# Moving the four feature-major projections of the gated linear attention from behind the delta rule's chain to between its silu gate and the first branch's norm

## The chip, the cores and the metric

One core of a Trainium2 chip. The metric is the device time of one execution in microseconds, the median of the runs shown. Engines are named as in the profile: PE (TensorE matmuls), DVE (VectorE), ACT (ScalarE), POOL (GpSimd), SP (the queue that issues most DMAs).

## The reference, cut to what matters

Two stacked blocks of two layers each, batch 1, 256 tokens, width 1024, all in float32. The change lies in the token mixing of the first block, which both of its layers run:

```python
def token_mixing(x, w_in, ...):
    h = (x @ w_in).astype(jnp.float32)
    h_rw, h_gla, h_gdn, h_gate = _split(h, GROUP_SPLITS)
    o_rw = rwkv7_time_mix(h_rw, ...)
    o_gla = gla_mix(q, k, v, gk_lo, gate, ...)         # the five parts of h_gla
    o_gdn = gated_deltanet_mix(qkv, a_in, b_in, gate, ...)
    branches = jnp.stack([o_rw, o_gla, o_gdn], axis=2)
    proj = jnp.einsum('btnc,ncd->btnd', branches, w_branch)
    gates = jax.nn.sigmoid(h_gate).reshape(B, T, N_BRANCH, D_MODEL)
    return jnp.sum(gates * proj, axis=2) @ w_o

def gla_mix(q, k, v, gk_lo, gate, gk_w2, gk_b, norm_g):
    log_a = jax.nn.log_sigmoid(gk_lo @ gk_w2 + gk_b) / GLA_GATE_NORM
    # per chunk of 64, b = cumsum(log_a):
    #   att[i, j] = sum_d q[i, d] k[j, d] exp(b[i, d] - b[j, d]),  j <= i
    #   o = att @ v + (q * exp(b)) @ S ;  S = S * exp(b_end) + (k * exp(b_end - b))^T v
    return _rms_norm(o, norm_g) * jax.nn.silu(gate)

def gated_deltanet_mix(...):
    # per chunk: t_inv = (I + lower)^-1 ; u = t_inv @ (v beta) ; w = t_inv @ (k beta exp(g))
    # chain over 4 chunks: v_new = u - w @ S ; o = (q exp(g)) @ S + att @ v_new ; S = ...
    return _rms_norm(o, norm_g) * jax.nn.silu(gate)
```

The second block (attention, then HGRN, each with a swiglu) is modulated by `silu(c) @ ada_w`, a matrix product that needs nothing of the first block.

## The kernel before

**Products.** Each float32 product is three matmuls of a high and a low part (hi·hi, hi·lo, lo·hi). The activations are split once per stage (`xh`, `xl`). Weights come in units of 128x1024 floats: SP loads `wr`, ACT makes `wh` (L78), DVE makes `wl` (L79). There are 4 buffers for `wr`, 4 for `wh` and 3 for `wl`. Feature-major projections ("fm", `fm_tile`, L102, L103 and L105) take one unit for one output tile of 128 features by 256 tokens, 24 matmuls. Token-major projections ("tm", L178 to L180) give 128 tokens by 512 features; a unit lasts for 12 matmuls when both halves of the tokens use it.

**Order.** The text gives an order of emission; a list scheduler then orders the instructions on each engine, so that two neighbouring steps of the text are interleaved where their dependences allow. Each engine runs its own list strictly in order.

**The stage.** `token_mix` emits in this order: 15 fm tiles for RWKV with its inverse and chain; 12 fm tiles for the delta rule (d15 to d26); `gd_mid`, in which the inverse of the delta rule is made (rounds on DVE L449/L450, transposes L455, copies on ACT L453 and L467 to tile `iz`, then four groups of L487 on PE with DVE between them); gate projections; the tm projection of the delta rule's silu gate (`silu_gate`, L951 to L953); the RWKV norm `rw_post` (DVE L697 to L704, PE L712/L713, DVE L714) and its output projection `proj(l, 0, ytm)`; the chain of the delta rule over four chunks (`gd_chain`, L895 to L927 with the head norm L937 to L944); then the gated linear attention: four fm tiles l27 to l30 (k and q, two tiles each, copied to `Lk`, `Lq` by ACT L962), `gl_mid`, the tm projection of v (`Lv`, L1201), and so on.

`gl_mid` works in two halves, j = 0 and 1. A half starts with L996 on PE (the decay gate, from data that are there long before) and the products of q and k (L1014, read by DVE L1015); DVE takes differences of the running sum (14 instructions, L975/L976), ACT one Exp of 128x1792 (L977), DVE multiplies by q and k (14 instructions, L981, tile `Lex`), and then, for seven levels, PE multiplies (L1025, four small matmuls into two `pt` tiles) and DVE copies the result under a mask into `Lat` (L1032, four of them). The `pt` tiles have two buffers, so level n+1 of L1025 cannot start before L1032 has read level n.

**Fill.** The projection of the second block's modulation is split into 48 doses. A dose is four matmuls (L1389) from a tile loaded ahead (`fr`) or from two `wr` tiles, with L1395, L1408 and L1414 behind every second one. Named places of the text (`spot`) fetch a tile ("f"), give a dose from a fetched one ("d") or give a number of doses. The places in question: `sg` f, `post` d, `chain` f, `l27` d, `l28` f, `l30` d, `lg` f, `g1` d, `p2` f, `glo` d, `wo0` f, `wo` d and 2 more.

Of the kernel before, what the change touches and what calls it, by code (L numbers as in the profile page):

```python
# [17 lines left out]
P = 128  # L18
T = 256
# [341 lines left out]
for _k, _w in ROWS:  # L361
# [3 lines left out]
FMT = (["lora"] + [f"{c}{p}" for p in range(4) for c in "krv"] + ["g0", "misc"]  # L365
       + [f"G{c}{h}" for c in "kqv" for h in range(4)] + ["Lk0", "Lq0", "Lk1", "Lq1"])
# [30 lines left out]
class Mix(Core):  # L397
# [557 lines left out]


    def gl_begin(self):
        self.lq = {c: self.t([P, 2, T], f"L{c}", bufs=1) for c in "kq"}

    def gl_tile(self, f, ps):  # L960
        j = int(f[2])
# [115 lines left out]
class Block(Mix):  # L1077
# [62 lines left out]
    def token_mix(self, l, pool, ln):  # L1140
        nc, tc = self.nc, self.tc
        self.wfm, self.wtm, self.layer = self.a["wfm"][l], self.a["wtm"][l], l
        self.merged, self.gt = {}, {}
        new = lambda n, **k: tc.tile_pool(name=f"{n}{l}", bufs=1, reuse_waits="tile", **k)
        with new("mg") as self.mg:
            self.pre = {(0, h): self.t([P, 2, 512], f"gate0{h}", pool=self.mg) for h in range(2)}
            self.vnat = self.t([P, 2, 512], "vnat", pool=self.mg)
            self.ytm = self.t([P, 2, 512], "ytm", pool=self.mg)
            self.load_params(l)
            with new("gd") as self.gd:  # L1150
                gw = ExitStack()
                self.gw = gw.enter_context(new("gw", side="right"))
                with new("gp") as self.gp:
                    self.rw_begin()
                    with new("mp") as self.mx:
                        for i in range(15):
                            self.rw_tile(i, self.fm_tile(i))
                            self.spot(f"r{i}")
                            if i == 14:
                                self.gates(0, self.mg, (0,))  # L1160
                    with new("mi") as self.mx:
                        self.rw_inverse()
                        self.rw_chain()
                with new("la") as self.late:
                    self.rt = self.t([P, NROW], "rt", pool=self.late)
                    self.gx = self.t([P, 1024], "gx", pool=self.late)
                    nc.gpsimd.dma_start(self.rt, self.a["row"][l:l + 1].broadcast_to([P, NROW]))
                    nc.gpsimd.dma_start(self.gx, self.a["gx"][l])
                    gs = self.t([P, 2, 512], "gsg", pool=self.late)
                    self.gd_begin()  # L1170
                    for i in range(15, 27):
                        self.gd_tile(FMT[i], i, self.fm_tile(i))
                        if i == 24:
                            self.gd_decay()
                        if i == 26:
                            self.gd_scale()
                        self.spot(f"d{i}")
                        if i == 18:
                            self.gates(0, self.mg, (1,))
                    with new("mj") as self.mx:  # L1180
                        self.gd_mid()
                    gw.close()
                    self.spot("mid")
                    self.gates(2, self.late)
                    self.spot("g2")
                    self.tm(self.wtm, 2 * KD, 1, self.xh, self.xl, KD, lambda n, t, ps: self.silu_gate(ps, gs[:, t], "gdn_g"), last=0)
                    self.spot("sg")
                    self.rw_post()
                    self.spot("post")
                    self.proj(l, 0, self.ytm)  # L1190
                    with new("dc") as self.dc:
                        self.gd_chain(lambda t, o: self.head_norm(o, gs[:, t], gs[:, t]))
                        with new("ml") as self.mx:
                            self.spot("chain")
                            self.gl_begin()
                            for i in range(27, 31):
                                self.gl_tile(FMT[i], self.fm_tile(i))
                                self.spot(f"l{i}")
                            self.gl_mid()
                            v = self.t([P, 2, 512], "Lv")  # L1200
                            self.tm(self.wtm, 0, 1, self.xh, self.xl, KD, lambda n, t, ps: nc.scalar.copy(v[:, t], ps), last=0)  # L1201
                            gl = self.t([P, 2, 512], "gsl")
                            self.tm(self.wtm, KD, 1, self.xh, self.xl, KD, lambda n, t, ps: self.silu_gate(ps, gl[:, t], "gla_g"), last=0)
                            self.spot("lg")
                            self.gates(1, self.mg)
                            self.spot("g1")
                            self.gl_out(lambda t: v[:, t], lambda t, o: self.head_norm(o, gl[:, t], gl[:, t]))
                            self.proj(l, 2, gs)
                            self.spot("p2")
                            self.spot("glo")  # L1210
                            self.proj(l, 1, gl)
            mh, ml = self.new_x("m")
            self.to_fm(lambda t: self.merged, mh, ml, scale=0.5)
        self.x_load(pool())
        self.ln_begin(ln)
        self.spot("wo0")
        self.tm(self.a["wo"][l], 0, 2, mh, ml, KD, self.ln_sink, cut=True)
        self.spot("wo")
        self.ln_end()
# [868 lines left out]
```

## Time and profile before

| what | value |
|---|---|
| median of 3 runs | 2869.21 us (2865.56 to 2870.39) |
| the profiled execution's own time | 2880.61 us |
| its span (first to last instruction) | 2878.4 us |
| mean granted clock of PE | 0.981 of full |
| PE busy | 2785.6 us, 97% of the span |
| DVE busy | 1879.9 us, 65% |
| ACT busy | 1299.4 us, 45% |
| chain that ended last | PE 85%, DVE 9%, ACT 3%, DMA 2% |

How to read it: the span less PE's busy time is what PE waits, 93 us over the whole execution. A matmul at half clock counts as busy, so time lost to the clock does not show in that difference; it shows in the granted clock of a stretch. In the first layer the silu gate of the delta rule ends at about 433 us of the span, the gated linear attention's last part at about 620; in the second layer it is the stretch from 1324 to 1510. All times below are of the profiled execution.

### The profile page before, as it was taken

To read this page: it belongs to the slowest core of one execution; us is meant where nothing else is said; L and a number is where in the kernel's file an instruction comes from. 1 tells how busy PE (TensorE), PEld (TensorE's weight loads), DVE (VectorE), ACT (ScalarE), POOL (GpSimd) and SP (SyncE) were. 2 spreads that over 40 slices of the span, in tenths; PEclk is the share of its full clock that TensorE was granted. 3 is DMA by queue.
4 is the path that set the end of the run, shared out by engine and by line. 5 is a ranking of instruction groups with operands and counts; after the bars stand their busy time and mean duration, and the time that the engine had idled before them with its cause. 6 is when DMAs were issued, how large, how long until landed. Compare 5 with 4: busy or idle time off the path is not lost.

```text
span 2878.4 us, 47877 instructions
## 1 busy us (share of the span) xinstructions
PE 2785.6 (97%) x18788; PEld 2457.3 (85%) x18788; DVE 1879.9 (65%) x3880; ACT 1299.4 (45%) x2040; POOL 202.8 (7%) x320
## 2 busy tenths in 40 slices
PE   8999999999999999999999998999999999999998
PEld 8978887669978987887778986798999888898897
DVE  5658885676556658877677657686444327799665
ACT  4436543435434435633444534564333225564543
POOL 0000220020000001211010001200000001000000
PEclk9999999899999999989999999999999999999999
DMA  7555333465556555323357556202322323214554
GB/s 251 182 196 172 115 127 103 140 210 188 185 205 216 183 186 188 128 97 118 117 181 240 180 179 218 100 8 89 97 98 93 125 93 117 76 57 155 182 182 151
DMA packets 117009, 426.64 MB, mean 148 GB/s; under 512 B 13600, under 2 KB 14112, under 8 KB 115760
## 3 DMA queue, kind: packets, MB, share of 16 engines
q1 hardware_dynamic: 115168, 419.01, 43.7%
q0 software_dynamic: 1472, 4.51, 0.5%
q8 instruction: 148, 2.42, 0.3%
q14 instruction: 77, 0.63, 0.1%
q10 hardware_dynamic: 144, 0.07, 0.0%
HBM read 420.36 MB, written 3.18 MB: 147 GB/s over the span
## 4 chain that ended last, share of the span: by engine, by line
PE 85%; DVE 9%; ACT 3%; DMA 2%; issue 1%; POOL 0%; DVEq 0%; POOLq 0%; ACTq 0%; SPq 0%
PE ps L102 13%; PE ps L103 13%; PE ps L105 12%; PE ps L179 10%; PE ps L178 10%; PE ps L180 10%; PE pc L487 2%; DVE wl L79 2%; PE pc L1389 1%; PE pc L1643 1%; PE pt L243 1%; PE pt L1025 1%; PE pt L1627 1%; ACT wh L78 1%; PE pt L1830 1%
## 5 line engine op out<-in xcount | busy, mean ns | idle before, releaser
L79 DVE TENSOR_TENSOR wl<-wr,wh 128x1024 fp32r<-128x1024 f32 x658 | 809.6, 1232 | 558.2 <-issue 199.4
L78 ACT CAST wh<-wr 128x1024 fp32r<-128x1024 f32 x658 | 688.2, 1048 | 670.8 <-PE ps L180 307.7
L102 PE MATMUL ps<-xh,wh 128*128 128x256 f32 x3280 | 940.3, 288 | 10.6 <-ACT xh L247 4.8
L103 PE MATMUL ps<-xh,wl 128*128 128x256 f32 x3280 | 933.9, 286 | 3.1 <-DVE wl L79 3.1
L105 PE MATMUL ps<-xl,wh 128*128 128x256 f32 x3168 | 902.6, 285 | 0.4 <-DVE xl L254 0.3
L102 PEld LDWEIGHTS ps<-xh,wh 128*128 128x128 f32 x3280 | 634.2, 193 | 21.8 <-ACT wh L78 6.0
L103 PEld LDWEIGHTS ps<-xh,wl 128*128 128x128 f32 x3280 | 633.8, 193 | 9.5 <-DVE wl L79 4.3
L105 PEld LDWEIGHTS ps<-xl,wh 128*128 128x128 f32 x3168 | 608.4, 192 | 5.9 <-issue 4.1
L178 PE MATMUL ps<-wh,xh 128*128 128x512 f32 (+1 forms) x624 | 248.5, 401 | 4.2 <-ACT wh L78 2.8
L179 PE MATMUL ps<-wl,xh 128*128 128x512 f32 (+1 forms) x624 | 249.5, 400 | 0.6 <-DVE wl L79 0.5
L180 PE MATMUL ps<-wh,xl 128*128 128x512 f32 (+1 forms) x624 | 247.2, 398 | 0.0
L180 PE MATMUL ps<-wh,hl 128*128 128x512 f32 (+1 forms) x616 | 228.7, 371 | 0.0
L179 PE MATMUL ps<-wl,hh 128*128 128x512 f32 (+1 forms) x616 | 228.5, 371 | 0.0
L178 PE MATMUL ps<-wh,hh 128*128 128x512 f32 (+1 forms) x616 | 228.2, 371 | 0.0
L178 PEld LDWEIGHTS ps<-wh,xh 128*128 128x128 f32 x624 | 119.4, 192 | 33.1 <-ACT wh L78 3.2
L179 PEld LDWEIGHTS ps<-wl,xh 128*128 128x128 f32 x624 | 119.9, 192 | 26.8 <-DVE wl L79 3.8
L180 PEld LDWEIGHTS ps<-wh,xl 128*128 128x128 f32 x624 | 119.8, 192 | 23.4 <-issue 1.1
L151 ACT ACTIVATE th<-ps 128x256 f32<-128x256 f32 x154 | 59.2, 384 | 171.0 <-PE ps L105 160.1
L178 PEld LDWEIGHTS ps<-wh,hh 128*128 128x128 f32 x616 | 116.1, 189 | 22.4 <-DVE g L154 0.4
L179 PEld LDWEIGHTS ps<-wl,hh 128*128 128x128 f32 x616 | 116.0, 188 | 21.6
L180 PEld LDWEIGHTS ps<-wh,hl 128*128 128x128 f32 x616 | 116.0, 188 | 21.4
L155 ACT CAST hh<-g 128x256 fp32r<-128x256 f32 x154 | 62.5, 406 | 116.9 <-DVE g L154 116.9
(565 smaller groups left out, 3736.7 us busy)
## 6 DMA issues: line engine op xcount, KB each, us to landing
wr<-in_up SPq DMA_DIRECT2D x264, 512.0 KB, 3.5
wr<-in_down SPq DMA_DIRECT2D x132, 512.0 KB, 3.4
wr<-in_wtm SPq DMA_DIRECT2D x72, 512.0 KB, 3.4
wr<-in_wfm SPq DMA_DIRECT2D x62, 512.0 KB, 4.0
fr<-in_ada SPq DMA_DIRECT2D x23, 1024.0 KB, 5.3
wr<-in_ada SPq DMA_DIRECT2D x38, 512.0 KB, 4.3
wr<-in_wbr SPq DMA_DIRECT2D x24, 512.0 KB, 3.5
wr<-in_whfm SPq DMA_DIRECT2D x24, 512.0 KB, 3.4
```

The lines of the kernel that those rows point to most:

```text
L78: on_act = nc.scalar.copy(hi, raw)
L79: on_dve = nc.vector.tensor_tensor(lo, raw, hi.bitcast(F32), ALU.subtract)
L102: nc.tensor.matmul(o, hi[:, w], xh[:, k], start=k == 0, stop=False)
L103: nc.tensor.matmul(o, lo[:, w], xh[:, k], start=False, stop=False)
L105: nc.tensor.matmul(o, hi[:, w], xl[:, k], start=False, stop=k == nk - 1)
L151: nc.scalar.activation(th, pa[:, :T], AF.Tanh, scale=0.5)
L155: nc.scalar.copy(hh[:, m], g)
L178: nc.tensor.matmul(o, xh[:, k, s], h, start=first, stop=False)
L179: nc.tensor.matmul(o, xh[:, k, s], l, start=False, stop=False)
L180: nc.tensor.matmul(o, xl[:, k, s], h, start=False, stop=end)
L243: nc.tensor.transpose(pt[:, j, t * P:t * P + P], self.cols(src(t), t, k + j), self.ident)
L487: nc.tensor.matmul(ps[:, 64 * u:64 * u + 64], lhs[:, u], rhs[:, u], start=True, stop=True)
```

## The change

The four fm tiles l27 to l30, with their spots, are emitted between spot `sg` and `rw_post` and no longer behind spot `chain`. Since the tiles `Lk` and `Lq` then live longer, they are taken from the pool `late`, which is open over both places, and no longer from the pool of the attention stage.

```diff
     def gl_begin(self):
-        self.lq = {c: self.t([P, 2, T], f"L{c}", bufs=1) for c in "kq"}
+        self.lq = {c: self.t([P, 2, T], f"L{c}", bufs=1, pool=self.late) for c in "kq"}
...
                     self.spot("sg")
+                    self.gl_begin()
+                    for i in range(27, 31):
+                        self.gl_tile(FMT[i], self.fm_tile(i))
+                        self.spot(f"l{i}")
                     self.rw_post()
                     self.spot("post")
                     self.proj(l, 0, self.ytm)
...
                             self.spot("chain")
-                            self.gl_begin()
-                            for i in range(27, 31):
-                                self.gl_tile(FMT[i], self.fm_tile(i))
-                                self.spot(f"l{i}")
                             self.gl_mid()
```

No instruction is added or taken away but for the doses' places. What the scheduler makes of it is shown at three places of the first layer; the second layer has the same pattern.

**Place A, PE, the inverse of the delta rule.** `pc` of L487 is its result, `iz` what it waits for, `ps_4856` the last tile of the silu gate. Before:

```order
L180 MATMUL ps_4856<-wh_4911,xl_2233 128x512
L712 MATMUL pt_4983<-gx_3669,g_537_3203 128x512
L713 MATMUL pt_4983<-gx_3669,misc_3241 128x512
L712 MATMUL pt_5031<-gx_3669,g_537_3203 128x512
L713 MATMUL pt_5031<-gx_3669,misc_3241 128x512
L487 MATMUL pc_4649<-iz_810_4635,int_4480 128x64 x8
L1414 MATMUL pt_5040<-cst,row_4473 128x128 x4
L243 MATMUL pt_5048<-cst,ytm_2280 128x128 x4
L487 MATMUL pc_4660<-iym_4648,ixb_4641 128x64 x8
```

After (`ps_4941` is tile l27, `ps_4984` tile l28):

```order
L180 MATMUL ps_4856<-wh_4911,xl_2233 128x512
L102 MATMUL ps_4941<-xh_2232,wh_4942 128x256
...
L105 MATMUL ps_4941<-xl_2233,wh_4942 128x256
L1414 MATMUL pt_4978<-cst,row_4473 128x128 x2
L487 MATMUL pc_4649<-iz_810_4635,int_4480 128x64 x8
L1414 MATMUL pt_4978<-cst,row_4473 128x128 x2
L102 MATMUL ps_4984<-xh_2232,wh_4985 128x256
...
L103 MATMUL ps_4984<-xh_2232,wl_4986 128x256
L487 MATMUL pc_4660<-iym_4648,ixb_4641 128x64 x8
L105 MATMUL ps_4984<-xl_2233,wh_4985 128x256
```

The 24 matmuls of l27 now stand ahead of the first L487 where the two pairs of L712/L713 stood; l28 to l30 stand behind it, between the four groups of L487, and L712/L713 follow them.

**Place B, PE, the levels of `gl_mid`, j = 0.** `ps_5830` and `ps_5831` are tiles of a tm projection, `pt` the results of a level. Before:

```order
L178 MATMUL ps_5830<-wh_5850,xh_2232 128x512
L179 MATMUL ps_5830<-wl_5851,xh_2232 128x512
L1025 MATMUL pt_5551<-Lex_5511 128x64 x2
L1025 MATMUL pt_5552<-Lex_5511 128x64 x2
L180 MATMUL ps_5830<-wh_5850,xl_2233 128x512
...
L180 MATMUL ps_5830<-wh_5850,xl_2233 128x512
L1025 MATMUL pt_5561<-Lex_5511 128x64 x2
L1025 MATMUL pt_5562<-Lex_5511 128x64 x2
L178 MATMUL ps_5831<-wh_5850,xh_2232 128x512
```

After (`fr` is a dose's tile):

```order
L178 MATMUL ps_5902<-wh_5904,xh_2232 128x512
L1025 MATMUL pt_5540<-Lex_5500 128x64 x2
L1025 MATMUL pt_5541<-Lex_5500 128x64 x2
L1025 MATMUL pt_5550<-Lex_5500 128x64 x2
L1025 MATMUL pt_5551<-Lex_5500 128x64 x2
L1025 MATMUL pt_5560<-Lex_5500 128x64 x2
L1389 MATMUL pc_6055<-fr_6243,adac 32x512
L1025 MATMUL pt_5561<-Lex_5500 128x64 x2
L179 MATMUL ps_5819<-wl_5840,xh_2232 128x512
L1025 MATMUL pt_5570<-Lex_5500 128x64 x2
```

Where seven tm matmuls stood between one level and the next, the levels now follow one another with one dose matmul between them, and the next tm row needs the weight part `wl_5840`.

**Place B, DVE.** `wl` is a low weight part, `Lat` the result of a level, `hss` to `rsy` the head norm of the delta rule's last chunk. Before:

```order
L981 TENSOR_TENSOR Lex_5511<-Lex_5511,Lk_5336 128x2x64
L1032 COPY_PREDICATED Lat_5485<-lvm,pt_5541 128x64 x2
L1032 COPY_PREDICATED Lat_5485<-lvm,pt_5542 128x64 x2
L1039 TENSOR_TENSOR Lke_5613<-Lke_5613,Lk_5336 128x128
L79 TENSOR_TENSOR wl_5869<-wr_5870,wh_5868 128x1024
L1032 COPY_PREDICATED Lat_5485<-lvm,pt_5551 128x32x2 x2
L1032 COPY_PREDICATED Lat_5485<-lvm,pt_5552 128x32x2 x2
L79 TENSOR_TENSOR wl_5887<-wr_5888,wh_5886 128x1024
```

After:

```order
L79 TENSOR_TENSOR wl_5822<-wr_5823,wh_5821 128x1024
L917 TENSOR_TENSOR go_947_5399<-goo_5442,pc_5437 64x512
L981 TENSOR_TENSOR Lex_5500<-Lex_5500,Lq_4940 128x128
...
L213 SCALAR_TENSOR_TENSOR rsy_5453<-rst_5454,rsy_5453 128x4
L1032 COPY_PREDICATED Lat_5474<-lvm,pt_5531 128x64
L944 SCALAR_TENSOR_TENSOR gsg_3672<-go_947_5399,rsy_5453,gsg_3672 128x128 x4
...
L1032 COPY_PREDICATED Lat_5474<-lvm,pt_5550 128x16x4 x2
L79 TENSOR_TENSOR wl_5840<-wr_5841,wh_5839 128x1024
L1032 COPY_PREDICATED Lat_5474<-lvm,pt_5551 128x16x4 x2
L1032 COPY_PREDICATED Lat_5474<-lvm,pt_5560 128x8x8 x2
```

Between two weight parts DVE now has the 14 L981, the head norm of the last chunk (L939 to L944) and the copies of two and a half levels; before, the head norm stood ahead of L981, and a weight part followed each level.

## Rows read from the trace of the kernel before

**Rows 1.** The page: its first line, and PE (busy us, share, instructions).

```profile
span 2878.4 us, 47877 instructions
PE 2785.6 (97%) x18788; PEld 2457.3 (85%) x18788; DVE 1879.9 (65%) x3880; ACT 1299.4 (45%) x2040; POOL 202.8 (7%) x320
```

**Rows 2.** Waits of PE, 390:620, then 1290:1520; us in total, times, longest.

```profile
PE pc L487 <- ACT iz L467: 5.0, 1, 5.0
PE pt L1025 <- ACT Lv L1201: 0.3, 1, 0.3
...
PE pc L487 <- ACT iz L467: 5.1, 1, 5.1
```

**Rows 3.** Timeline of PE from the silu gate's end: start, us, instruction, [wait, releaser].

```profile
433.07 0.39 PE L180 MATMUL ps<-wh,xl 128*128 128x512 f32 x1
433.30 1.02 PE L712 MATMUL pt<-gx,g 128*128 128x512 f32 x2
...
436.36 1.12 PE L713 MATMUL pt<-gx,misc 32*128 32x512 f32 x2
442.44 3.65 PE L487 MATMUL pc<-iz,int 128*128 128x64 f32 x16 [4.96 <-ACT iz L467]
```

**Rows 4.** Stretches: length, PE, PEld, DVE, ACT, POOL busy (x), PEclk, DMA share, GB/s.

```profile
442.44:449.07 6.63, 6.63 (x32) 6.63 (x32) 3.19 (x6) 2.09 (x4) 0.00 (x0) 0.50 0.01 2
534.40:551.30 16.90, 16.90 (x44) 10.83 (x43) 5.21 (x15) 6.65 (x10) 0.00 (x0) 0.50 0.20 66
...
1424.00:1432.00 8.00, 8.00 (x34) 5.15 (x33) 2.69 (x11) 2.35 (x4) 0.00 (x0) 0.79 0.21 68
```

**Rows 5.** Timeline of PE: neighbouring fm matmuls, and a level between tm matmuls.

```profile
654.06 0.28 PE L102 MATMUL ps<-xh,wh 128*128 128x256 f32 x1
654.18 0.28 PE L103 MATMUL ps<-xh,wl 128*128 128x256 f32 x1
...
532.03 0.50 PE L179 MATMUL ps<-wl,xh 128*128 128x512 f32 x1
532.46 0.66 PE L1025 MATMUL pt<-Lex 64*128 64x64 f32 x4
533.05 0.50 PE L180 MATMUL ps<-wh,xl 128*128 128x512 f32 x1
```

**Rows 6.** Timeline of DVE in the head norm and in `gl_mid`, j = 0.

```profile
506.73 0.68 DVE L939 TENSOR_REDUCE hss<-sgt 128x4 f32<-128x512 f32 x1
...
508.38 0.15 DVE L211 TENSOR_TENSOR rst<-rsy 128x4 f32<-128x4 f32 x1
...
508.65 0.15 DVE L212 SCALAR_TENSOR_TENSOR rst<-rst,hss 128x4 f32<-128x4 f32 x1
...
512.82 1.14 DVE L944 SCALAR_TENSOR_TENSOR gsg<-go,rsy,gsg 128x128 f32<-128x128 f32 x4
...
516.90 2.35 DVE L79 TENSOR_TENSOR wl<-wr,wh 128x1024 fp32r<-128x1024 f32 x2
519.17 0.28 DVE L981 TENSOR_TENSOR Lex<-Lex,Lq 128x128 f32<-128x128 f32 x1
...
522.00 0.73 DVE L1032 COPY_PREDICATED Lat<-lvm,pt 128x64 f32<-128x64 uint8 x4
```

**Rows 7.** Groups of ACT by form, 433:620: busy us, mean ns, idle before.

```profile
L977 ACT ACTIVATE Lex<-Lex 128x1792 f32<-128x1792 f32 x2 | 3.4, 1698 | 0.0
L903 ACT COPY gvn<-pc 64x512 f32<-64x512 f32 x4 | 2.3, 580 | 4.6 <-PE pc L901 4.6
```

**Rows 8.** Timeline of PE: a dose in the next norm, that norm's longest wait, and the HGRN head's end.

```profile
640.63 1.42 PE L1389 MATMUL pc<-wr,adac 128*32 128x512 f32 x5
...
648.01 0.58 PE L102 MATMUL ps<-xh,wh 128*128 128x256 f32 x1 [2.78 <-ACT xh L247]
...
2639.63 1.05 PE L243 MATMUL pt<-cst,o 128*128 128x128 f32 x4 [1.96 <-DVE o L1854]
...
2641.68 0.63 PE L178 MATMUL ps<-wh,xo 128*128 128x512 f32 x1
```

## The prediction

> **What bounds the kernel now.** I read the page first: PE is busy 97% of the span [rows 1], so a change that adds and removes no matmul can move the time in three ways only: PE waits for something else, the same matmuls run at another clock, or small matmuls break runs of large ones in other places. Then the waits of PE in the stage. In the first layer's stage there is one large wait, 5.0 us, at the first L487 of the delta rule's inverse, released by ACT's copy to `iz`; the second layer has the same with 5.1; the levels of `gl_mid` (L1025) wait only 0.3 us [rows 2]. The timeline shows the first: the silu gate's last matmul starts at 433.07, L712/L713 fill until 437.5, and L487 starts at 442.44 [rows 3]. Last I read the granted clock by stretches, because a slow matmul counts as busy: after that wait PE runs at 0.50, the lower level of 1.2 GHz, for 6.63 us, all of it busy, which loses 3.3 us; and from 534.40 to 551.30, at the end of `gl_mid` and behind it, it runs 16.90 us at 0.50, which loses 8.5. The second layer loses less there: 8.00 us at 0.79, which is 0.21 x 8.00 = 1.7 us [rows 4].
>
> **The change, part by part.** All sums stand against the profiled execution, 2880.61 us (span 2878.4 [rows 1], 2.2 outside it). The median of the runs shown is 2869.21, so a result of mine is multiplied by 2869.21/2880.61 = 0.996.
>
> *The wait at the inverse (place A).* What frees it is DVE's chain of rounds and ACT's copies; the order on DVE and ACT ahead of `iz` is the same in both kernels, so L487 stays at about 442.4. In front of it PE had L712/L713, from 433.30 to about 437.5, 4.2 us [rows 3]. Now it has l27 alone: 24 fm matmuls at 0.12 us from one start to the next [rows 5] are 2.9, with two L1414 about 3.2. The wait grows by 1.0, in each of the two layers: +2.1 us. l28 to l30 stand behind L487, where PE waited for nothing, and the L712/L713 that they push back are no longer cover for anything. DVE's L714, which now follows them, releases L243; I put 0.2 a layer on that, from nothing to the 0.7 that one such DVE instruction takes by the like of L939 [rows 6]: +0.4. The half clock behind the wait stays, since the wait does: 0.
>
> *Small groups between large matmuls.* A tm matmul in front of a level takes 0.43 us from start to start instead of 0.23 (532.03 to 532.46 [rows 5] against 433.07 to 433.30 [rows 3]). With l27 to l30 joined to other fm and the levels joined to each other, the order has 121 passages from large to small matmuls or back in the first layer's stage before and 115 after, and 125 and 116 in the second. At 0.1 each, half of those 0.20, the 15 fewer give −1.5 (0 to −3).
>
> *The levels of `gl_mid` (place B).* Before, `gd_chain` ran over the fm tiles and the levels over the tm projection of v. Now the chain and the first half of `gl_mid` share one place, the chain uses up v, and the levels stand together, with DVE's weight part `wl_5840` behind two and a half of them. I count from PE's last L901 of the chain in the first layer. ACT: L903 0.58, a rest of L916 about 0.3, Exp L977 1.70 [rows 7]: 2.7 with the hand-over. Then DVE: 5 L981 at 0.20 (14 from 519.17 to 522.00), L939 0.68, 9 pairs of an L981 and a row of the norm at 0.27 (508.38 to 508.65), 3 pairs of an L1032 and such a row, also at 0.27, four L944 1.14, 7 more L1032 at 0.18, L1039 about 0.2, L79 1.13 (two in 519.17 − 516.90) and the 2 L1032 that a level ahead of the tm row still wants, 0.4 [rows 6]: 9.0, so 11.7 in all. PE has in the same time 20 tm matmuls (4.6), 4 L909 and 14 L1025 at 0.15 (four in 532.46 to 533.05 [rows 5]; 2.7), 5 matmuls of a dose at 0.28 (1.4 [rows 8]) and four passages into small groups (0.8): 9.5. PE waits 2.2 us. The second layer, counted from its last L909: DVE 0.7 + 3 L981 0.6 + 3 L1032 0.5 + L939 0.7 + 12 pairs 3.2 + L944 1.1 + 3 L1032 0.5 + L1039 0.2 + L79 1.1 = 8.7; PE 4 tm 0.9 + 18 L1025 2.7 + 8 dose matmuls 2.2 + passages 0.4 = 6.2; it waits 2.5. The second halves (j = 1) have `gsl`'s gating (L952/L953) between levels and the weight part behind them; by the same durations DVE and PE come out within 1 us of each other: 1.0 and 0.5. Each hand-over between the two engines that my sums leave out adds, and I take 0.9 for all. Together 7.1, less the 0.6 of before: +6.5. The low bound is 0 (DVE finds room between the levels and PE waits as before [rows 2]); the high one is 16, if DVE's busy times are added in place of the distances of their starts. Who is late next: behind `wl_5840` DVE has a weight part every second level, 1.5 us for 2.7 us of PE, so it catches up.
>
> *The clock in `gl_mid`.* 8.5 + 1.7 us are lost there now. In the changed order the waits come earlier, and dense tm matmuls follow them. I take one low stretch in each layer like the one at place A, 6.6 us and 3.3 lost each [rows 4]: 6.6 less 10.2 = −3.6. The bounds are no loss at all, −10.2, and the long stretch of 16.90 us in both layers, 17.0 less 10.2 = +6.8. The trace does not tell what begins such a stretch: at 2641.7 tm matmuls take 0.63 us right behind a wait of 1.96 us [rows 8], while the long one began where PE had no wait.
> The Trainium skill, "TensorE: Matmul & The Clock Gate", Part 1 on the HAM clock gate, says that the default state is throttled and that activity releases the throttle; by that rule busy PE time is what keeps the clock up. The trace agrees for place A, where the low clock follows 4.96 us of wait [rows 3], and does not for the 16.90 us that were busy throughout at 0.50 [rows 4].
>
> *Doses.* 48 stay, at about 1.1 us each (5 matmuls in 1.42 [rows 8]), but they change places: the first layer's stage has 6 now and 4 then, the norm behind it 2 and 4, the second layer's stage one fewer, and the end of the HGRN head 4 and 6. In the norm PE waits 2.78 us for `xh`, and at the head's end 1.96 [rows 8]; two more doses of 2.2 fit roughly into each. I take −0.6. If the norm takes them and the end as well, it is −2; if at the end they hold the tm weights back by the four `wr` buffers that they fill, +5.
>
> Sum: 2.1 + 0.4 − 1.5 + 6.5 − 3.6 − 0.6 = +3.3, so 2883.9 for the profiled execution and 2872.5 for the median.
>
> **The rivals.** *R1, the long half clock in both layers.* The levels stand together now, and small fp32 matmuls next to waits are where the clock fell at 534.40. If both layers then run 16.90 us at 0.50, the clock term is +6.8 in place of −3.6: +13.7, 2894.3, or 2883. For it: the fall without any wait. Against: the second layer now has 3.4 us of it in the same place. It decides from 4.8 us of half clock more than I assume, 2.4 us lost, which lift the sum over 5.7. *R2, DVE stays ahead.* The weight parts lie far enough ahead that the levels wait 0.6 as before, and the clock behaves as before: 2.1 + 0.4 − 1.5 − 0.6 = +0.4, or 2869.6. For it: three buffers of `wl`. Against: all three are filled ahead of L917, and none between L917 and the third level. *R3, the fm tiles fill the wait at the inverse*, as their new place in the text would let one think: the 5.0 + 5.1 us and the half clock behind them (3.3, and I put the same in the second layer) go, so −16.7 replaces +2.5, in all −15.9, 2864.7, or 2854.5. Against it: only l27 stands ahead of L487, and the engine that ends the wait keeps its order. For it: the scheduler's order would allow it if `iz` came earlier than I think. *R4, the clock stays up in `gl_mid`*: the waits are cut into pieces by levels, so PE never rests for long, and nothing is lost there: 3.3 − 6.6 = −3.3, 2877.3, or 2865.9. Against it: the stretch from 534.40.
> R4 is what the rule of the Trainium skill's page "TensorE: Matmul & The Clock Gate" (Part 1, the HAM clock gate) would give for a PE that is kept active.
>
> **How the numbers follow.** Two kernels that differ by less than 0.2%, 5.7 us, can't be told apart by a measurement here. Chances: my forecast 0.46, of which 0.25 lies within 5.7 us, 0.20 above and 0.01 below (its own range is 2865 to 2881); R1 0.20, slower; R2 0.13 and R4 0.07, both within; R3 0.08, faster; 0.06 for a gain that I don't see, from the doses or the clock elsewhere. So slower 0.20 + 0.20 = 0.40, same 0.25 + 0.13 + 0.07 = 0.45, faster 0.01 + 0.08 + 0.06 = 0.15. The predicted time is that of the forecast, 2872.5. The range reaches down to 2859, which leaves out R3, and up to 2887, past R1 and most of the high bound of the waits.
>
> **What would show it.** Place A: a wait of about 6 us at L487 from ACT's `iz`, still near 442.4, with l27 ahead of it, and the half clock behind it; a wait below 2 us says R3. Place B: waits of 2 to 3 us on L1025 or L179 in the first half of `gl_mid`, released by DVE's `Lat` (L1032) or `wl` (L79), in both layers; 0.3 says R2. The clock there: about 6.6 us at 0.50 in each layer; 17 says R1, none R4. The 2.78 us in the norm shrink. I am wrong if the weights themselves come late (waits on L78 or SP), which no row of before shows, or if the chain of the delta rule, now filled with tm matmuls of 0.23 us in place of fm of 0.12, waits for DVE that has `gl_mid` to do between its steps.

## The result and the profile after

The changed kernel takes 2898.63 us (2888.21 to 2907.80), the kernel before in the same comparison 2869.61: a ratio of 1.0104 [1.0087, 1.0122]. It is slower by 29 us, 26 more than forecast and 12 past the upper end of the range. The profiled execution took 2888.21 us, the lowest of the four. The page of after, to be held against [rows 1]:

```profile
span 2886.3 us, 47870 instructions
PE 2783.5 (96%) x18788; PEld 2445.6 (85%) x18788; DVE 1883.6 (65%) x3880; ACT 1299.9 (45%) x2040; POOL 199.1 (7%) x320
```

PE's busy time is 2.1 us less and the span 7.9 more: 10.0 us of new waits. But this compares a low execution of after with a high one of before (2880.61 against a median of 2869.21). For a fair comparison I split every run, since each comes with its span and its mean granted clock: the *full-clock time* is span x clock, about what the execution would take with the same waits if the clock never fell, and the *clock loss* is the rest of the span. The clock has three decimals, so one run's split is good to 1.4 us. The means:

| | runs | median us | full-clock time | clock loss (range) |
|---|---|---|---|---|
| before | 77 | 2869.2 | 2824.2 | 43.7 (37 to 58) |
| after | 4 | 2898.6 | 2831.9 | 64.5 (55 to 73) |

So some 8 us are waits and 21 are clock. Place A in after, PE from the end of l27 (columns: start, us, instruction, [wait, releaser]):

```profile
433.36 0.38 PE L1414 MATMUL pt<-cst,row 128*128 128x128 f32 x2
439.71 3.65 PE L487 MATMUL pc<-iz,int 128*128 128x64 f32 x16 [5.97 <-ACT iz L467]
```

The wait is 5.97 us where it was 4.96 [rows 3], and L487 at half clock behind it takes the same 3.65. The waits of PE over both stages, 390:625 and then 1290:1520, against [rows 2] (us in total, times, longest):

```profile
PE pc L487 <- ACT iz L467: 6.0, 1, 6.0
...
PE pc L1389 <- DMA fr<-in_ada: 1.7, 1, 1.7
PE ps L180 <- DVE bl L248: 1.0, 1, 1.0
PE ps L178 <- ACT bh L247: 0.9, 2, 0.5
PE ps L178 <- ACT xh L247: 0.6, 1, 0.6
PE pt L1025 <- DVE Lke L1039: 0.5, 1, 0.5
...
PE ps L179 <- DVE wl L79: 0.4, 1, 0.4
...
PE pc L487 <- ACT iz L467: 5.7, 1, 5.7
PE ps L178 <- ACT bh L247: 1.4, 2, 1.0
...
PE pt L1025 <- DVE rst L211: 0.7, 1, 0.7
```

The waits for `bh`, `bl` and `xh` (activations that the last projections of the stage read) stand at the end of each layer's stage, where before had 0.3 us for `bh` in each layer. With the smaller ones beside them they add some 5 us.

Far from both places, at the start of the second block's attention, stands a difference that the prediction has no step for. PE there, before and then after:

```profile
1789.11 0.60 PE L1414 MATMUL pt<-cst,row 128*128 128x128 f32 x4
1790.38 1.06 PE L1389 MATMUL pc<-wr,adac 128*32 128x512 f32 x8 [0.67 <-ACT row L1395]
1791.38 0.66 PE L1414 MATMUL pt<-cst,row 128*128 128x128 f32 x4
1794.37 0.79 PE L179 MATMUL ps<-wl,xc 128*128 128x512 f32 x1 [2.33 <-DVE wl L79]
```

```profile
1782.39 0.62 PE L178 MATMUL ps<-wh,xh 128*128 128x512 f32 x2
1782.94 1.02 PE L1408 MATMUL pt<-row,adasum 128*2 128x512 f32 x2
1789.19 0.79 PE L179 MATMUL ps<-wl,xc 128*128 128x512 f32 x1 [5.22 <-DVE wl L79]
```

Before, a dose (its four matmuls are eight records) and the L1414 of two pairs stood in front of the wait for `wl`; after, only one pair's L1408 stands there and the wait is 5.22 us. The clock of the stretch around it, before and after (length, busy time of PE, PEld, DVE, ACT, POOL, PEclk, DMA share, GB/s):

```profile
1755.00:1900.00 145.00, 135.80 (x763) 109.06 (x762) 105.67 (x233) 69.70 (x126) 32.64 (x26) 0.99 0.33 111
```

```profile
1755.00:1900.00 145.00, 132.38 (x708) 103.50 (x706) 98.84 (x220) 66.62 (x123) 29.81 (x27) 0.95 0.31 103
```

PE waits 12.6 us there in place of 9.2, and the clock loss is 7 us in place of 1.5.

### The profile page after: what moved, and what is told of

Same layout as the page of the kernel before. It is cut to its first block, busy times and chain, and to the rows that moved or that the text cites. A ratio compares the mean times of both kernels' runs of the same rounds, so it can differ in the third digit from the quotient of the medians.

```text
span 2886.3 us, 47870 instructions
## 1 busy us (share of the span) xinstructions
PE 2783.5 (96%) x18788; PEld 2445.6 (85%) x18788; DVE 1883.6 (65%) x3880; ACT 1299.9 (45%) x2040; POOL 199.1 (7%) x320
## 4 chain that ended last, share of the span: by engine, by line
PE 84%; DVE 10%; ACT 3%; issue 2%; DMA 1%; POOL 0%; DVEq 0%; POOLq 0%; SPq 0%; ACTq 0%
PE ps L102 13%; PE ps L103 13%; PE ps L105 12%; PE ps L179 10%; PE ps L180 10%; PE ps L178 10%; DVE wl L79 2%; PE pc L487 2%; PE pc L1389 1%; PE pc L1643 1%; PE pt L243 1%; ACT wh L78 1%; PE pt L1830 1%; PE pt L1025 1%; PE pt L1627 1%
## 5 line engine op out<-in xcount | busy, mean ns | idle before, releaser
L179 PE MATMUL ps<-wl,xh 128*128 128x512 f32 (+1 forms) x624 | 252.3, 404 | 2.4 <-DVE wl L79 2.4
L179 PE MATMUL ps<-wl,hh 128*128 128x512 f32 (+1 forms) x616 | 228.1, 370 | 0.0
L179 PEld LDWEIGHTS ps<-wl,xh 128*128 128x128 f32 x624 | 120.1, 193 | 31.4 <-DVE wl L79 6.5
L179 PEld LDWEIGHTS ps<-wl,hh 128*128 128x128 f32 x616 | 115.7, 188 | 21.9
```

The lines of the kernel that those rows point to most:

```text
L179: nc.tensor.matmul(o, xh[:, k, s], l, start=False, stop=False)
```

## The experiments

The theories at the start were the forecast's (waits at the levels of place B), R1's (half clock at the levels) and, from the rows just shown, the doses. The change does three things at once: it puts small work behind the inverse's wait (place A), takes the projections away in front of the levels (place B), and moves the four spots, by which the plan of doses comes out differently. The first runs undo one at a time. All of these kernels compute the whole result.

**again**: the changed kernel once more, unedited.

> The changed kernel once more, unchanged. In its first four runs it took 2888 to 2908 us, and span times granted clock (2886.3 x 0.981, 2898.2 x 0.978, 2895.2 x 0.977, 2905.8 x 0.975) is 2829 to 2834 us in all four, so what differs between them is the clock. Theory CLOCK (the changed order makes PE fall to half clock more often): again 2888 to 2908, mean clock 0.975 to 0.981, and the kernel before beside it 2865 to 2871 with a clock about 0.985. Rival CHIP (the first runs met a chip or an hour with a lower clock for any kernel): 2875 to 2880, 7 to 10 over the kernel before, which is what waits and passages alone come to.

It took 2899.84 us, 1.0102 [1.0086, 1.0119], clock loss 59.1 (52 to 67). The loss is the change's and no accident of the first executions. Its profile (2898.9 us of span) is nearer to the median than the first, and shows the levels of the second layer, PE in 1406:1418 and then the clock:

```profile
1406.77 0.67 PE L1025 MATMUL pt<-Lex 64*128 64x64 f32 x8
1408.11 1.06 PE L1025 MATMUL pt<-Lex 64*128 64x64 f32 x8 [0.67 <-DVE rst L211]
1409.35 1.06 PE L1025 MATMUL pt<-Lex 64*128 64x64 f32 x8 [0.18 <-DVE rst L212]
1410.59 0.63 PE L1025 MATMUL pt<-Lex 64*128 64x64 f32 x4 [0.18 <-DVE rsy L213]
1411.87 1.91 PE L1389 MATMUL pc<-fr,adac 128*32 128x512 f32 x2 [0.65 <-DMA fr<-in_ada]
1413.72 1.13 PE L1025 MATMUL pt<-Lex 64*128 64x64 f32 x8
1414.77 1.93 PE L1389 MATMUL pc<-fr,adac 128*32 128x512 f32 x6
```

```profile
1411.00:1438.00 27.00, 26.35 (x71) 15.21 (x71) 12.48 (x35) 6.12 (x8) 0.00 (x0) 0.51 0.38 135
1438.00:1442.00 4.00, 4.00 (x17) 3.24 (x16) 4.00 (x14) 3.10 (x4) 0.00 (x0) 0.88 0.10 38
```

Three and a half levels stand in a row, with three short waits; then a dose waits 0.65 us for its own load, and from there PE runs 27 us at half clock although it is busy for 26.35 of them: 13 us lost. These four waits together are 1.7 us. The page shows nothing of this; the granted clock of the stretch does. But the row of levels alone does not bring it: the profiled execution of after, with the same instructions and waits of 0.67, 0.18, 0.18 and 0.33 us, ran the same stretch at 0.91:

```profile
1411.00:1438.00 27.00, 27.00 (x121) 16.53 (x119) 19.27 (x61) 12.25 (x16) 0.00 (x0) 0.91 0.44 156
```

**spots_back**: the projections early as in the change, the spots in their old place.

```diff
                     for i in range(27, 31):
                         self.gl_tile(FMT[i], self.fm_tile(i))
-                        self.spot(f"l{i}")
                     self.rw_post()
...
                             self.spot("chain")
+                            for i in range(27, 31):
+                                self.spot(f"l{i}")
                             self.gl_mid()
```

> The projections are moved as in the change, but the four spots l27 to l30 stay behind the chain, so the doses keep nearly their old places. If the doses' new places (in the norm, in the attention's start and at the end of the HGRN head) cost the time: 2870 to 2880. If the moved projections themselves do it: within 5 us of the changed kernel.

2872.5 us, 1.0010 [0.9997, 1.0023]: not told apart from before, with place A as in the change. Clock loss 39.4. The wait at attention is 2.65 us, and the levels of the second layer keep the clock but for some 3 us:

```profile
1790.13 0.50 PE L179 MATMUL ps<-wl,xc 128*128 128x512 f32 x1 [2.65 <-DVE wl L79]
```

```profile
1401.00:1411.00 10.00, 9.48 (x54) 5.92 (x53) 8.11 (x38) 3.27 (x4) 0.00 (x0) 1.00 0.57 202
1411.50:1415.00 3.50, 3.50 (x14) 2.41 (x15) 1.49 (x3) 0.00 (x0) 0.00 (x0) 0.57 0.95 304
```

So the early projections alone cost little (the interval reaches to 7 us); most of the 29 come only when the spots move along.

**early_two**: l27 and l28 early, l29 and l30 behind the chain, each with its spot.

```diff
                     self.gl_begin()
-                    for i in range(27, 31):
+                    for i in range(27, 29):
...
                             self.spot("chain")
+                            for i in range(29, 31):
+                                self.gl_tile(FMT[i], self.fm_tile(i))
+                                self.spot(f"l{i}")
                             self.gl_mid()
```

> Only l27 and l28 are emitted early, l29 and l30 behind the chain as before. Place A (the wait at the inverse) is then as in the change, L487 waits about 6 us in each layer; the chain of the delta rule keeps fm tiles as fill, and the levels of gl_mid keep tm matmuls between them. If place A costs the time: within 5 us of the changed kernel. If place B (the levels in a row): 2870 to 2876.

2875.48, 1.0029 [1.0017, 1.0040]. Its full-clock time is that of `again` (2835.1 to 2835.2), its clock loss 38.3. This is what was expected if place A is not the cost. Its levels stand between token-major matmuls again, if not in the order of before, and the stretch of the first layer in which before lost 8.5 us [rows 4] runs at full clock:

```profile
450.00:640.00 190.00, 186.07 (x980) 132.46 (x978) 127.43 (x334) 74.06 (x115) 17.00 (x16) 1.00 0.45 155
```

So levels that stand apart need not lose these 8.5 us, which the forecast had counted as something to be won. That they are no property of the order before is argued from this, not shown: only one execution of before was profiled.

**after_proj**: the four projections with their spots behind `proj(l, 0, self.ytm)`, so that place A is as before and, in the first layer, place B as after.

```diff
                     self.spot("sg")
+                    self.rw_post()
+                    self.spot("post")
+                    self.proj(l, 0, self.ytm)
                     self.gl_begin()
...
-                    self.rw_post()
-                    self.spot("post")
-                    self.proj(l, 0, self.ytm)
```

> All four projections are emitted behind the first branch's output projection and ahead of the delta rule's chain. Place A is then word for word as in the kernel before (L487 waits 5.0 and 5.1 us), place B as in the change (ten L1025 in a row). If place B costs the time: within 5 us of the changed kernel. If place A: 2870 to 2876.

2889.5, 1.0080 [1.0067, 1.0094], clock loss 60.6, full-clock time 2825.7. This meets neither expectation: some 10 of the 29 us go, all of the full-clock time, and the whole clock loss stays. It does not tie the 10 us to place A, where L487's longer waits are 1.6 us in sum, nor the clock loss to place B: in the second layer the levels do not stand in a row here, and run at full clock, while 17 us of half clock lie ahead of them, in the delta rule's chain:

```profile
1356.00:1373.00 17.00, 17.00 (x53) 10.56 (x53) 4.74 (x11) 4.80 (x10) 0.00 (x0) 0.50 0.10 41
1393.00:1448.00 55.00, 54.93 (x282) 36.54 (x281) 40.02 (x139) 22.46 (x32) 0.00 (x0) 1.00 0.39 136
```

**spots_only**: the kernel before with nothing but the four spots moved to behind `sg`.

```diff
                     self.spot("sg")
+                    for i in range(27, 31):
+                        self.spot(f"l{i}")
                     self.rw_post()
...
                                 self.gl_tile(FMT[i], self.fm_tile(i))
-                                self.spot(f"l{i}")
```

> The projections stay where the kernel before has them; only the four spots l27 to l30 are emitted early, behind the silu gate. The stage then gives three doses a layer in place of four (spot post finds no fetched tile, spot lg finds one already fetched), so the later doses slide by two, and two more stand at the end of the HGRN head, as in the change. Theory LOST DOSES (the sliding of the doses costs the time): 2885 to 2900, clock 0.978 to 0.982. Rival EARLY DOSES (doses among the levels of gl_mid cost it) and rival PROJECTIONS: 2866 to 2874.

2880.29, 1.0037 [1.0023, 1.0051]: without a single projection moved, some 10 us are lost, which lies between the ranges of both theories. Most of it is full-clock time (2831.7; the clock loss is 46.0). At attention L179 waits 6.03 us for `wl`. The reason can be read in the plan: with the spots ahead of `post`, `post` finds no fetched tile and gives no dose, and `lg` finds one already there and fetches none. Each layer's stage loses a dose; all later doses slide back by as many places, and two end up in the flush at the end of the HGRN head.

**lost_doses**: spots_back, but l27 gives no dose; nothing else is moved.

```diff
-PLAN=dict(... chain='f',l27='d',l28='f', ...)
+PLAN=dict(... chain='f',l28='f', ...)
```

> As spots_back (projections early, spots late, 2872.5 us), but the plan's entry l27 gives no dose, so that one dose a layer is lost to the stage and slides to the end of the HGRN head, while no dose comes earlier. LOST DOSES: 2885 to 2900. EARLY DOSES: 2868 to 2876.

2876.38, 1.0023 [1.0011, 1.0034], again between the ranges (LOST DOSES missed by 9 us, EARLY DOSES by less than one). The rows at attention are those of after, with projections and later spots as in spots_back:

```profile
1771.85 1.02 PE L1409 MATMUL pt<-row,adasum 128*2 128x512 f32 x2
1777.81 0.80 PE L179 MATMUL ps<-wl,xc 128*128 128x512 f32 x1 [4.95 <-DVE wl L79]
```

```profile
1755.00:1900.00 145.00, 132.62 (x728) 104.96 (x727) 98.95 (x218) 70.58 (x129) 29.51 (x26) 0.95 0.27 90
```

This settles that the lost doses make the wait at attention: it is 4.95 to 6.43 us in the five kernels that lose them (after, again, after_proj, spots_only, lost_doses) and 2.3 to 3.9 in the nine others. In four of the five the stretch loses 7 us to the clock, in after_proj 3, in the others 0 to 3. What they cost in all is less sure: some 4 us against spots_back here, where the two intervals overlap, and some 10 in spots_only against before. They are a part of the 29 and not the whole.

**plan_kept** and **none_lost**: the change, with the plan mended so that no dose is lost. plan_kept:

```diff
-PLAN=dict(... post='d',chain='f',l27='d', ...)
+PLAN=dict(... post='f',chain='d',l27='d', ...)
```

none_lost, where the doses behind the stage are also those of before:

```diff
-PLAN=dict(... post='d',chain='f',l27='d',l28='f',l30='d',lg='f', ...)
+PLAN=dict(... post='f',l27='d',l28='f',l30='d',lg='df', ...)
```

> The whole change, but with the plan's entries post and chain exchanged (post fetches, chain gives a dose), so that each layer's stage again gives four doses and none slides behind the stage. LOST DOSES: 2868 to 2877, clock 0.985 to 0.988. EARLY DOSES or PROJECTIONS: 2885 to 2900.

> The whole change with the plan's entries post, chain and lg written so that no dose is lost to the stage (post fetches, chain does nothing, lg gives a dose and fetches). The first layer's place B is then word for word as in the change (ten L1025 in a row, doses between them), and behind the stage every dose stands as in the kernel before, none at the end of the HGRN head. Theory SUM (levels in a row with doses among them, and lost doses, each cost on their own): about 2880, clock loss about 49 us as in plan_kept (2881 mean, 48.5), the wait at the attention's start back from 5 to 6 us to 2.3 to 2.8. If lost doses alone carry the change's cost: 2870 to 2875. If place B alone: 2890 to 2900.

2882.24, 1.0039 [1.0025, 1.0054], and 2887.71, 1.0060 [1.0037, 1.0083]. Both lie between what was expected if the lost doses were all of it and if they were nothing of it; none_lost is 8 us over the 2880 that the sum of two costs gave. The wait at attention is mended in none_lost (2.35 us), but what the doses cover there is not the whole loss. In plan_kept's second layer the levels stand in no long row (doses and token-major matmuls lie between them); PE waits 1.02 us for a weight part, and from 2 us later some 27 us at half clock follow in which it waits for nothing:

```profile
1808.42 0.50 PE L179 MATMUL ps<-wl,xc 128*128 128x512 f32 x1 [2.35 <-DVE wl L79]
```

```profile
1410.82 0.50 PE L178 MATMUL ps<-wh,xh 128*128 128x512 f32 x1 [1.02 <-ACT wh L78]
```

```profile
1412.00:1440.00 28.00, 28.00 (x81) 18.81 (x80) 10.18 (x28) 5.54 (x8) 0.00 (x0) 0.52 0.32 119
```

The first row is none_lost's, the others plan_kept's. With these the clock losses make a square: projections and spots not both early, and no dose lost, 43.7 (before) and 39.4 (spots_back); doses lost alone 46.0 (spots_only) and 43.4 (lost_doses); projections and spots both early and none lost 48.5 (plan_kept) and 53.8 (none_lost); both 59.1 to 64.5 (after, again, after_proj). By these means, of 4 to 12 runs each but for before, there are two losses, and together they are more than their sum.

Where the second one sits is only in part seen. At the levels of both layers, from the first L1025 to the last, the traces have 27 us of half clock in after, 44 in again, 41 in plan_kept and 24 in none_lost, but 7 in after_proj; the nine other traces have 0 to 21. Each is a single execution, so that early doses and projections together bring more half clock to the levels is borne out, and which feature of the order does it is not shown.

The remaining runs ask what R3 had promised: can the projections fill the inverse's wait?

**fill28**: spots_back, and the first L487 may not stand ahead of the last matmul of l28.

```diff
                         self.gl_tile(FMT[i], self.fm_tile(i))
+                        if i == 28:
+                            self.behind(self.inv_ops[0], self.fm_last)
```

> As spots_back, with one order edge more: the first matmul of the inverse (L487) is to stand behind the last matmul of l28 on PE, so that two fm tiles (5.8 us) and not one stand ahead of it. In spots_back the wait there should be about 6 us as in the change. If iz comes as before: the wait falls to 3 us, the half clock behind it shrinks or goes, and the kernel takes 2860 to 2868. Rival: l28 needs a PSUM tile that DVE frees only at about 440 us (L952 of the silu gate), so PE waits there in place of at L487, and the time is that of spots_back, 2869 to 2875.

2875.14, 1.0012 [0.9998, 1.0026], the rival's time. The wait only goes elsewhere:

```profile
440.20 0.35 PE L102 MATMUL ps<-xh,wh 128*128 128x256 f32 x1 [4.11 <-DVE sgt L953]
...
444.64 1.89 PE L488 MATMUL pc<-iz,int 128*128 128x64 f32 x16
```

l28 needs the PSUM tile from which DVE takes the silu gate, and DVE is at that until 440.2; L487 (L488 here) starts 2 us later than before. It then runs at full clock, 1.89 us where before had 3.65, and the kernel is not faster for it.

**fill_sg2**, **fill_sg3**, **fill_sg4**: two, three or four of the projections ahead of the silu gate's own matmuls, L487 behind the last of those; the other projections and all spots as before. The edit of fill_sg2 (the others have 30 and 31 in place of 29):

```diff
+                    self.gl_begin()
+                    for i in range(27, 29):
+                        self.gl_tile(FMT[i], self.fm_tile(i))
                     self.tm(self.wtm, 2 * KD, 1, ..., last=0)
+                    self.behind(self.inv_ops[0], self.tm_last)
                     self.spot("sg")
```

> l27 and l28 alone are moved, to ahead of the silu gate's tm projection, l29, l30 and all spots stay, and an order edge puts the first L487 behind the silu gate's last matmul. Two fm tiles (5.8 us) then stand ahead of L487 more than in the kernel before, less the L712/L713 (4.2 us) that move behind it, and unlike in fill28 no PSUM tile of the silu gate is awaited by an fm tile. Expected: the 5 us wait falls below 3.5 and the half clock behind it to 3.4 to 6.8 us of half clock from 10.2; 2858 to 2866. Rival: DVE's weight parts for the two units come in front of iz and put it off by as much: 2868 to 2875.

> As fill_sg2 with all four fm tiles ahead of the silu gate: 11.5 us ahead of L487, less 4.2. No wait for iz at L487, no half clock behind it; but the delta rule's chain then runs over tm v, as in the change, and the levels stand closer: full-clock time about 10 us below spots_back (2830), clock loss 30 to 35 us; 2852 to 2864. Rival: L487 comes later than iz, so the chain's start waits for the inverse, and nothing is won: 2868 to 2875.

> As fill_sg2 and fill_sg4, with l27 to l29 ahead of the silu gate and l30 in the chain, all spots late. fill_sg2 waited 3.17 us at L487 and then ran at half clock for 30.7 us over the small groups in a row behind it; fill_sg4 ran the same groups in a row without a wait ahead of them and kept the clock. With three tiles (8.6 us, less the 4.2 of L712/L713) the wait should be about 0.5. Theory (the wait lets the clock fall, and small groups in a row keep it down): no half clock in this stage's place A, full-clock time 2822 to 2826, clock loss 36 to 42, 2860 to 2870. Rival (small groups in a row let the clock fall by themselves): half clock of 20 us and more behind L487 in both layers as in fill_sg2, 2880 to 2890.

2885.94, 1.0062 [1.0039, 1.0084]; 2869.90, 0.9998 [0.9982, 1.0015]; and 2872.58, 1.0006 [0.9987, 1.0025], for two, four and three. The first is above both ranges that were expected, the second has the time of its rival and the rows of its forecast. PE at the first L487 of fill_sg2 and the clock behind it:

```profile
442.55 3.64 PE L488 MATMUL pc<-iz,int 128*128 128x64 f32 x16 [3.17 <-ACT iz L468]
```

```profile
443.00:470.50 27.50, 27.03 (x94) 18.63 (x95) 11.03 (x18) 4.62 (x8) 1.04 (x2) 0.50 0.10 34
```

and the same small groups in fill_sg4:

```profile
443.40 1.89 PE L488 MATMUL pc<-iz,int 128*128 128x64 f32 x16
...
447.75 1.97 PE L488 MATMUL pc<-iym,ixb 128*128 128x64 f32 x16 [0.50 <-DVE iym L497]
```

```profile
443.40:458.80 15.40, 14.43 (x96) 10.12 (x94) 11.78 (x18) 4.35 (x7) 1.04 (x2) 1.00 0.35 103
```

With four tiles ahead the wait is gone, and the same small groups run at full clock in about half the time. fill_sg3 decides nothing between its theory and its rival: no wait at the first group, but 1.81 us at the second, and half clock behind that, as its rival had it, while its time lies between the two ranges:

```profile
448.26 2.93 PE L488 MATMUL pc<-iym,ixb 128*128 128x64 f32 x16 [1.81 <-DVE iym L497]
```

```profile
448.30:470.00 21.70, 21.23 (x80) 15.47 (x81) 8.95 (x16) 2.13 (x5) 1.04 (x2) 0.53 0.13 40
```

fill_sg4 thus does what R3 wanted, and the median is still that of before: its full-clock time is 2825.0, its clock loss 41.1 (26 to 52). In its profiled execution the mixing stages lose next to nothing to the clock, but the second layer's RWKV part, 1140:1300, runs at a mean of 0.93 and loses 11 us. The profiled execution of before has 0.93 there too, that of after 0.99, and none of the edits touches that part. What the stage gives is thus of the size of what the clock takes elsewhere from one trace to the next. The lowest execution of fill_sg4 took 2854.63. None of these kernels is faster than the one before by more than its interval.

## Why the prediction was wrong, step by step

*The wait at the inverse: right.* L487 waits 5.97 and 5.71 us, forecast 6; l27 is the only tile ahead, and the half clock behind it is as before. A slip without effect: R3's 2864.7 scales to 2853.3, not 2854.5. Its cause (the chain that ends in ACT's `iz`) holds: R3 does not happen by itself, and fill28 shows that it would not if forced from there. Only with the tiles ahead of the silu gate (fill_sg4) does it.

*The waits of the levels: too large.* Forecast 7.1 us; the rows of after give 0.54 + 0.37 + 0.41 + 0.32 in the first layer and 0.67 + 0.18 + 0.18 + 0.33 in the second, 3.0. The releasers are the DVE steps of the sum (`Lat`, `Lke`, `wl`, the head norm's `rst`, `gsl`'s gating). The sum itself was wrong on PE's side. The order's eight L487 are sixteen records in the trace [rows 3], and the four L1025 of a level are eight; 0.15 us is the price of a record [rows 5], and I took it for each L909 and L1025 of the order, which take 0.30. With that PE has 12.2 us of work in the first layer and 8.9 in the second, against 11.7 and 8.7 on DVE, and no wait comes of it; the 3.0 that were measured are not explained by this sum. Not named were the dose that follows too closely behind its own fetch (1.73 us for `fr`) and the waits at the end of both stages, some 5 us. Most of these stand in spots_back, too, so they come with the projections' new place rather than the doses'; no run here takes them apart.

*The doses: the first step that failed.* "48 stay, but they change places" is true, and −0.6 for them was wrong in sign: the spots alone cost some 10 us (spots_only). I looked at the places where doses arrive and not at those that they leave. A dose is cover for an in-order wait; what left the attention's start cost 3.4 us of wait and some 5.5 of clock in the profiled execution. In the norm the gain that I had put did come. Beside the 2.78 us [rows 8] before had these waits there, 4.9 in all:

```profile
643.86 0.44 PE L243 MATMUL pt<-cst,x 128*128 128x128 f32 x2 [1.22 <-DVE x L291]
644.79 0.44 PE L243 MATMUL pt<-cst,x 128*128 128x128 f32 x2 [0.49 <-DVE x L291]
...
649.22 0.87 PE L102 MATMUL ps<-xh,wh 128*128 128x256 f32 x2 [0.41 <-ACT wh L78]
```

After, one of 3.43 is left, inside the dose:

```profile
647.52 1.45 PE L1408 MATMUL pt<-row,adasum 128*2 128x512 f32 x2 [3.43 <-ACT row L1395]
```

*The clock at the levels: the second, and the largest.* I took −3.6: 10.2 us won back, and one short low stretch in each layer. What I took back was read from one execution. early_two and spots_only, whose levels stand apart as well, run the first layer's at 1.00; fill28, where they stand closer, has 17 us at half clock there again. And the levels of both layers got 27 us of half clock in after and 44 in `again`, so 14 and 22 us lost against the 10.2 of the profile before: +3 and +12 where I had −3.6. That is R1's size, and its cause is not shown: the same row of levels ran at 0.91 in one execution and at 0.51 in another. R1 had a chance of 0.20, and its sum of 2883 had the same false credit of 10.2 us in it; without it and with the doses' 9 us it comes to 2902, a sum made afterwards from single executions.

*The baseline: the third.* The profiled execution of before was 11 us above its median. I scaled that away by 0.996 for the whole time, but the difference sat in the clock: its mean was 0.981, and most other executions of before have 0.984 to 0.987. A term that is read from such a profile may be the very excess that the median doesn't have; the 8.5 us at the levels may be, and so may the 11 us of the second layer's RWKV part, of which the prediction has nothing. Held against each other, the two profiled executions differ by 7.6 us, forecast 3.3, and none of it is clock (54.7 and 54.8 us lost): a high one of before met the lowest of after.

The sum by what the runs show: the waits of PE in the trace add up to 83.1 us before and 92.7 after, so 9.6 more: 1.6 (L487) + 2.4 (levels, 3.0 less the 0.6 of before) + 1.7 (`fr`) + 5.0 (the stages' ends) + 3.4 (attention) − 1.5 (the norm) − 3.0 (elsewhere, some 5 less in the other norms and 2 more at single places). The split of the runs gives 8, that of `again` 11. My terms other than the clock come to 6.9, and that this is near is luck: the levels were 4 too large, and the stages' ends, the attention and the gains in the norms, which I did not have, nearly make up for it. The rest, 15 to 21 us, is clock, where I forecast −3.6; of it the trace of `again` has 12 more than that of before at the levels and 5 to 6 more at attention.

*What stays open:* why the clock falls in one execution and not in the next of the same order (after varies from 55 to 73 us of loss, with the same instructions, its levels from 0.91 to 0.51, and the RWKV part of the second layer from 0.93 to 0.99 between kernels whose text is the same there), where the clock loss of after_proj sits, why spots_back and early_two have 6 and 11 us more full-clock time than before when L487's longer waits are 2 of them, and why the two losses together are more than their sum. No run here tells that.

## What to carry to other kernels

When background work is placed by named points in the text, a moved point takes its work along, and every later place changes: follow the whole list to the program's end and ask at each place that loses some what it covered. Read the granted clock by stretches in more than one execution before a low stretch is counted as something to be won. And look at the granted clock behind small dependent groups with waits among them: here waits of 0.2 to 1 us were followed by 27 us at half clock in two traces, and by 7 in a third, which had the instructions of one of them, so such a place is a risk and not a fixed price. When a sum counts matmuls of the program at a price read from the trace, check first how many records one of them makes.

## What the runs showed of the hardware

The half clock outlasted its occasion. In fill_sg2 PE was busy for 27.03 of 27.50 us and had 0.50 throughout; in fill_sg4 the same groups without the wait of 3.17 us in front had 1.00. In `again` the last rows of the low stretch are token-major matmuls in a row, at first at half clock too, and the clock rose among them (0.88 in 1438:1442). The Trainium skill, "TensorE: Matmul & The Clock Gate", Part 1 on the HAM clock gate, says that activity releases the throttle; if activity is the profile's busy time, these rows don't agree with that, since PE was busy for 0.98 of the stretch at half clock and for 0.94 of the one at full clock. What I had not expected either is the spread: one program, the changed kernel, ran with mean clocks from 0.975 to 0.981 in its first four executions, 2888 to 2908 us, a range as wide as two thirds of the change's whole effect.
